# Hybrid attention block: gate weights prepared in a written order inside the last norm, and the norm's root in 128x1 pieces

## The chip, the cores and the metric

The kernel runs on one core of one Trainium2 chip. The metric is device microseconds of one execution. Five engines work side by side, each in its own program order: TensorE (matrix products, PE in the rows; its weight loads are PEld), VectorE (DVE), ScalarE (ACT), GpSimd (POOL) and SyncE (SP). Here SP does nothing but start loads, and POOL starts most stores.

## The reference, cut to what matters

One block: a mixer (short convolution and attention, merged and projected by `w_out`), then a SwiGLU feed-forward net. Each is normalised before and after. 1024 rows of 1024 columns, all float32.

```python
x = x + rmsnorm(m, norm_mix_post)            # m: the mixer's output
h = rmsnorm(x, norm_ffn_pre)
gu = einsum("bsd,df->bsf", h, w_gate_up)     # 1024 x 5632
g, u = split(gu, 2)
f = einsum("bsf,fd->bsd", silu(g) * u, w_down)
x = x + rmsnorm(f, norm_ffn_post)
```

`rmsnorm(x, g)` is `x * rsqrt(mean(x*x) + 1e-6) * g`, row by row.

## The kernel before, in words

**Products.** Each float32 operand is split into a high and a low part (`split`: ScalarE copies the high part, tile `hi`; VectorE subtracts it, tile `lo`), and a product is three matrix products, hi*hi, hi*lo and lo*hi (`mm3`). Each large product is a Strassen scheme over halves; `prod` is one of its terms: 4 blocks, 12 matrix products of 128x512.

**The place of the change.** After the mixer, the rows are worked off in four pairs of 128-row tiles (i = 0 to 3). `first`, `second`, `p_s1` to `p_a22` make the output of `w_out`; `e_norm(i)` does the post-norm, adds to x, stores x and does the pre-norm of the net; `e_turn(i)` transposes the two normalised tiles on TensorE (tile `tp`), and ScalarE copies them to `um`, from where `half_split` and `h2_sums` make the operands of the gate products. In `e_norm` the first tile of a pair lies in `raw` (pairs 0 to 2) or `keep` (pair 3), the second in `tt`. ScalarE squares each tile and sums it (`ssq`), then takes the root (`sq`); VectorE makes the inverse root of both tiles at once in `rms_finish`, on 128x2 values: a reciprocal, two multiplications, and a last step.

**The gate weights.** The columns of `w_gate` come in blocks of 128. Of eleven of them (`FIRSTS`, here called gate weights 0 to 10) the first two Strassen terms are done early, `f_begin` and `f_end`; this work stands around the last norm so that TensorE has something to do while VectorE normalises. The program writes `begin_early(0)`, `e_turn(2)`, `begin_early(1)`, `end_early(0)`, ..., `e_turn(3)`, then a loop over weights 4 to 10. A weight is loaded by SP into one of three `raw` buffers (weight 1 into `sx`), and split into `hi` and `lo`. The three `raw` buffers hold the pairs' tiles before, so a load waits until the buffer's last user is done:

```python
def raw_t():
    return wtile("raw", 3)
def prep_first(src1, there=None):
    if there is None:
        r1 = raw_t()
        nc.sync.dma_start(r1, kmaj(src1))
        h1, l1 = hi_t(), lo_t()
        split(h1, l1, r1)
```

In the loop, at weight 8, the lower half of the normalised rows is split into `hch` (ScalarE, in written order) and `hcl` (VectorE), four pieces each.

**What sets the order.** A scheduler orders each engine's instructions, except those that are made within `pinned(call, engine)` or under `strict[0]`: these are kept in the written order on that engine. The scheduler also decides which instructions of TensorE stand between others where they are not pinned. All work of VectorE and ScalarE goes through helpers, so every row of the profile says L77.

Of the kernel before, what the change touches and what calls it, by code (L numbers as in the profile page):

```python
# [13 lines left out]
ALU = mybir.AluOpType  # L14
# [33 lines left out]
def block_kernel(  # L48
# [20 lines left out]
    class InOrder:  # L69
# [15 lines left out]
    nc = SimpleNamespace(  # L85
        **{e: InOrder(e) for e in engines}
    )
# [22 lines left out]
    def add(o, a, b):  # L110
        nc.vector.tensor_tensor(o, a, b, op=ALU.add)

    def sub(o, a, b):
        nc.vector.tensor_tensor(o, a, b, op=ALU.subtract)
# [4 lines left out]
    def pinned(call, *names):  # L119

        was, strict[0] = strict[0], names
        call()
        strict[0] = was
# [5 lines left out]
    def copy(o, a):  # L129
        nc.scalar.activation(o, a, AF.Copy)  # L130

    def split(hi, lo, src):

        copy(hi, src)
        sub(lo, src, f32(hi))
# [9 lines left out]
    cpool, _ = pool("const")  # L145
    stat, _ = pool("stat", 4, side="right")
    stat.tile([P, 56], F32, name="pad", bufs=1)
    dpool, _ = pool("dram", space=DRAM)
# [34 lines left out]
    def rms_scale(ssq, rest=None, tile_=st_tile, w=1):  # L183
        return rms_finish(*rms_root(ssq, rest, tile_, w), tile_, w)

    def rms_root(ssq, rest=None, tile_=st_tile, w=1):

        va, sq = (tile_(n, w) for n in ("va", "sq"))
        eps = -0.5 * EPS if rest is None else rest[1]
        nc.vector.tensor_scalar(va, ssq, -0.5 / D, eps, op0=ALU.mult, op1=ALU.add)  # L190
        if rest is None:
            nc.scalar.activation(sq, va, AF.Sqrt, scale=-2.0)
        else:
            nc.scalar.activation(sq, ssq, AF.Sqrt, scale=1.0 / D, bias=rest[0])
        return va, sq
# [226 lines left out]
    op0, rest0 = upper(0, tp0)  # L422
# [36 lines left out]
    op1, rest1 = upper(1, tp1)  # L459
# [40 lines left out]
    for st in range(2, ST):  # L500
# [12 lines left out]
        if st + 3 == ST:  # L513
            ax_close()
            w0, w0_close = pool("w0", side="right")
            r0, h0, l0 = w0_tiles()
# [16 lines left out]
    wpool, _ = pool("w")  # L533
# [7 lines left out]
    def wtile(tag, bufs, dt=F32, shape=(P, KT, P)):  # L541
        return wpool.tile(list(shape), dt, tag=tag, name=tag, bufs=bufs)

    def raw_t():
        return wtile("raw", 3)

    def hi_t():
        return wtile("hi", 4, F32R)

    def lo_t():  # L550
        return wtile("lo", 3, F32R)
# [10 lines left out]
    def kmaj(src):  # L562
        return src.rearrange("(k p) m -> p k m", p=P)
# [3 lines left out]
# [7 lines that stand above are left out]
        else:  # L574
            r1, h1, l1 = there
        return dict(A11=(h1[:, LO], l1[:, LO]), A12=(h1[:, UP], l1[:, UP])), r1
# [469 lines left out]
    for ij, (kind, j, _, _) in enumerate(jobs):  # L1046
        work = side.pop(ij, [])

        def mid():
            for cut, _ in work:  # L1050
                pinned(cut, "vector", "scalar")
# [7 lines left out]
        if ij < 2:  # L1059
            if ij == 0:  # L1060
                r1 = raw_t()
# [13 lines left out]
            w = {**w, **prep_rest(wcols(jobs[ij][3]), r1)}  # L1075
            if ij == 1:
                pairs.q.append(pairs.prep(*pairs.srcs.popleft()))
            _, c12, c21, c22 = strassen(w, h1b, psm, pp, p1, mid)
        elif ij < len(jobs) - 1:
# [3 lines left out]
            w = pairs.get()  # L1083
# [3 lines left out]
        else:  # L1087
            w = pairs.get()
# [14 lines left out]
        elif kind == "gb":  # L1103
            for m, parts in ((j, (c11, c12)), (j + 1, (c21, c22))):
                zt = zts.pop(m)
                for n in range(2):
# [5 lines left out]
                    for t in (1, 0):  # L1112
# [5 lines left out]
                            op0=ALU.mult, op1=ALU.add,  # L1118
# [337 lines left out]
    PAIRS = ST // 2  # L1456
# [106 lines left out]
    for u in range(4):  # L1563
# [3 lines left out]
    late = [  # L1567
        x for t in (wtile("raw", 3), wtile("sx", 1)) for x in kept_halves(flat(t))
    ]
    late = {u: [gate(2 * u + 1 - x, n2, late.pop(0)) for x in range(2)] for u in (3, 0)}  # L1570
# [54 lines left out]
    gpr = bcast_row(norm_ffn_pre[0], ep, name="gpr")  # L1625

    def st2(name, bufs=2):
        return ep.tile([P, 2], F32, tag=name, name=name, bufs=bufs)

    def scale2(ssq):  # L1630
        return rms_scale(ssq, None, lambda n, w: st2(n), 2)

    def square(src, acc):
        junk = ep.tile([P, NC], F32, tag="junk", name="junk")
# [2 lines left out]
    sx = wtile("sx", 1)  # L1637
# [72 lines left out]
        prod(b1s[i], rests[i]["A22"], wob[T4], False)  # L1710
        square(b1s[i], qas[i][:, 1:2])

    def e_norm(i):
        qa = qas[i]
        add(qa, qa, qbs[i])
        rs = scale2(qa)
        tt = keeps[i], ep.tile([P, D], F32, tag="t", name="tt", bufs=1)
        xp = [xts.popleft() for _ in range(2)]
        ssq = st2("ssq")
        for e, parts in enumerate(  # L1720
            (((slice(0, D), keeps[i]),), ((n1, b1s[i]), (n2, c22s[i])))
        ):
            for ns, c in parts:
                nc.vector.scalar_tensor_tensor(
                    tt[e][:, ns], c, rs[:, e : e + 1], gpo[:, ns], op0=ALU.mult, op1=ALU.mult
                )
            add(xp[e], xp[e], tt[e])
            rows_ = slice((2 * i + e) * P, (2 * i + e + 1) * P)
            nc.gpsimd.dma_start(x2_dram[rows_, :], xp[e])
            nc.scalar.activation(tt[e], xp[e], AF.Square, accum_out=ssq[:, e : e + 1])  # L1730
        rs = scale2(ssq)
        for e in range(2):
            nc.vector.scalar_tensor_tensor(
                tt[e], xp[e], rs[:, e : e + 1], gpr, op0=ALU.mult, op1=ALU.mult
            )
            if 2 * i + 3 + e < ST:
                xts.append(load_xt(2 * i + 3 + e))
        turned.append(tt)
# [29 lines left out]
    def f_src(f):  # L1768
        return wgu[:, f * P : (f + 1) * P], wgu[:, FH + f * P : FH + (f + 1) * P]

    FIRSTS = [*range(2, NPRE), 0, 1]
    begun, kept, aside = {}, {}, {}

    def f_begin(n, b1, p1):
        f = FIRSTS[n]
        w, _ = prep_first(f_src(f)[0], aside.get(n))
        prod(b1, w["A11"], hb[B11], True)
        pinned(lambda: copy(p1, b1), *(("scalar",) if n >= 8 else ()))
        if f > 1:
            nc.gpsimd.dma_start(pre_dram[f][0], p1)  # L1780
        begun[n] = w, b1, p1
# [35 lines left out]
    for i in range(PAIRS):  # L1817
        if i + 1 < PAIRS:
            rests.append(rest_ops(i + 1))
        if i:  # L1820
            p_s1(i)
        p_s3(i)
        if i > 1:
            e_turn(i - 2, (0,))
        if i + 1 < PAIRS:
            p_s2(i + 1)
        if i > 1:
            e_turn(i - 2, (1,), (0,))
        if i == 3:
            p_a22(i)  # L1830
        if i > 1:
            e_turn(i - 2, (1,), (1,))
            half_split(B11, i - 2)
        if i == 2:
            hb.append(both(x_tile(2)))
        if i > 1:
            half_split(B21, i - 2)
        for p_ in ((p_a22, p_s4), (p_s4, p_a22), (p_s4, p_a22), (p_s4,))[i]:
            p_(i)
        e_norm(i)  # L1840
    hb.append(None)
    hb += [both(x_tile(n, p)) for n, p in ((0, wx), (3, wx), (4, wy), (5, wy))]
    r_, h_, l_ = wtile("sx", 1), hi_t(), lo_t()
    nc.sync.dma_start(r_, kmaj(f_src(FIRSTS[1])[0]))
    split(h_, l_, r_)
    aside[1] = r_, h_, l_
    sx = flat(wtile("sx", 1))
    early = [sx[:, n1], sx[:, n2], t_(fe, "c22"), t_(fe, "c22")]

    def begin_early(f):  # L1850
        if f == 2:
            raw_t()
        f_begin(f, pk.tile([P, NC], F32, tag="p1", name="b1"), early[f])

    def end_early(f):
# [605 lines left out]
```

## Time and profile before

| | |
|---|---|
| median of 3 runs | 1312.46 us (1311.39 to 1313.31) |
| profiled execution | 1312.72 us, its span 1311.0 us |
| granted clock of TensorE | 0.998 of full speed over the span |
| busy, share of the span | TensorE 99%, weight loads 83%, VectorE 74%, ScalarE 47%, GpSimd 12% |
| chain that ended last | TensorE 93%, VectorE 3%, DMA 2%, ScalarE 1% |

The stretch of the change lies between about 630 and 745 us of the span. From 650 to 745 us the page's rows show a full clock throughout. "Busy" of TensorE counts the modelled length of products that overlap, so waits shorter than an overlap don't show there; they show as the distance from one start to the next, which is 0.227 us where 128x512 products follow each other.

### The profile page before, as it was taken

To read this page: it belongs to the slowest core of one execution; us is meant where nothing else is said; L and a number is where in the kernel's file an instruction comes from. 1 tells how busy PE (TensorE), PEld (TensorE's weight loads), DVE (VectorE), ACT (ScalarE), POOL (GpSimd) and SP (SyncE) were. 2 spreads that over 40 slices of the span, in tenths; PEclk is the share of its full clock that TensorE was granted. 3 is DMA by queue.
4 is the path that set the end of the run, shared out by engine and by line. 5 is a ranking of instruction groups with operands and counts; after the bars stand their busy time and mean duration, and the time that the engine had idled before them with its cause. 6 is when DMAs were issued, how large, how long until landed. Compare 5 with 4: busy or idle time off the path is not lost.

```text
span 1311.0 us, 18265 instructions
## 1 busy us (share of the span) xinstructions
PE 1300.0 (99%) x6776; PEld 1087.4 (83%) x6776; DVE 964.0 (74%) x1501; ACT 611.0 (47%) x985; POOL 154.9 (12%) x289
## 2 busy tenths in 40 slices
PE   9999999999999999999999999999999999999997
PEld 8988888888888888888888888888888888888886
DVE  6975979875656877588798767777776667676685
ACT  6642423243355866454677434433343334444452
POOL 0001100011112222011012111211100110000000
PEclk9999999999999999999999999999999999999999
DMA  6347657668646544589466555543323338866441
GB/s 218 114 121 225 188 171 209 177 217 231 190 137 209 162 138 138 164 316 376 148 211 208 160 169 176 184 155 105 104 83 112 110 115 308 315 236 198 154 162 65
DMA packets 207242, 235.15 MB, mean 179 GB/s; under 512 B 12064, under 2 KB 150368, under 8 KB 207152
## 3 DMA queue, kind: packets, MB, share of 16 engines
q1 hardware_dynamic: 159136, 156.08, 37.8%
q0 software_dynamic: 18832, 63.22, 13.3%
q10 hardware_dynamic: 29184, 14.68, 4.5%
q8 instruction: 53, 0.87, 0.3%
q14 instruction: 37, 0.30, 0.1%
HBM read 161.79 MB, written 72.16 MB: 178 GB/s over the span
## 4 chain that ended last, share of the span: by engine, by line
PE 93%; DVE 3%; DMA 2%; ACT 1%; issue 1%; SPq 0%; DVEq 0%; ACTq 0%
PE b L77 54%; PE pd L77 16%; PE pba L77 3%; PE pv L77 3%; PE tps L77 3%; PE po L77 3%; PE p L77 2%; PE sp L77 2%; PE pbp L77 2%; PE pbv L77 1%; PE zb L77 1%; DMA xt<-in_x_dram 1%; PE ma L77 1%; PE q L77 1%; PE tp L77 1%
## 5 line engine op out<-in xcount | busy, mean ns | idle before, releaser
L77 PE MATMUL b<-x,hi 128*128 128x512 f32 x1088 | 335.6, 390 | 0.0
L77 PEld LDWEIGHTS b<-x,hi 128*128 128x128 f32 x1088 | 203.4, 188 | 42.0 <-ACT c L77 0.2
L77 PE MATMUL b<-x,lo 128*128 128x512 f32 x544 | 212.0, 390 | 0.0
L77 DVE TENSOR_TENSOR lo<-raw,hi 128x1024 fp32r<-128x1024 f32 (+1 forms) x89 | 107.1, 1203 | 48.6 <-PE b L77 39.4
L77 ACT ACTIVATE hi<-raw 128x1024 fp32r<-128x1024 f32 (+1 forms) x95 | 96.4, 1017 | 87.4 <-PE b L77 58.6
L77 PEld LDWEIGHTS b<-x,lo 128*128 128x128 f32 x544 | 102.1, 188 | 21.5 <-DVE lo L77 0.3
L77 DVE TENSOR_TENSOR c<-c,b 128x512 f32<-128x512 f32 x111 | 75.6, 682 | 29.6 <-PE b L77 21.3
L77 ACT ACTIVATE hi<-sx 128x1024 fp32r<-128x1024 f32 (+1 forms) x43 | 44.8, 1042 | 101.1 <-PE b L77 84.7
L77 DVE TENSOR_TENSOR sx<-raw 128x512 f32<-128x512 f32 x78 | 53.7, 688 | 24.8 <-DMA raw<-in_w_gate_up_dram 12.6
L77 DVE TENSOR_TENSOR lo<-sx,hi 128x1024 fp32r<-128x1024 f32 (+1 forms) x43 | 51.5, 1198 | 27.4 <-PE b L77 24.2
L77 PE MATMUL pd<-hi,lo 128*128 128x512 f32 x160 | 62.3, 389 | 0.0
L77 PE MATMUL pd<-hi 128*128 128x512 f32 x160 | 61.9, 390 | 0.0
L77 DVE TENSOR_TENSOR um<-um,b 128x512 f32<-128x512 f32 x47 | 31.9, 685 | 37.2 <-PE b L77 36.7
L77 PE MATMUL pd<-ghi 128*128 128x512 f32 x148 | 57.7, 390 | 0.0
L77 PE MATMUL pd<-glo,ghi 128*128 128x512 f32 x148 | 57.6, 389 | 0.0
L77 PE MATMUL pd<-ghi,glo 128*128 128x512 f32 x148 | 57.6, 389 | 0.0
L77 ACT ACTIVATE c<-b 128x512 f32<-128x512 f32 x49 | 28.9, 594 | 61.4 <-PE b L77 61.2
L77 PE MATMUL b<-hT34h,lo 128*128 128x512 f32 x136 | 52.9, 389 | 0.0
L77 PE MATMUL b<-hT12h,lo 128*128 128x512 f32 x136 | 52.9, 389 | 0.0
L77 PE MATMUL b<-hT34l,hi 128*128 128x512 f32 x136 | 52.9, 389 | 0.0
L77 PE MATMUL b<-hT12l,hi 128*128 128x512 f32 x136 | 52.9, 389 | 0.0
L77 PE MATMUL b<-hT34h,hi 128*128 128x512 f32 x136 | 52.9, 389 | 0.0
(505 smaller groups left out, 3166.2 us busy)
## 6 DMA issues: line engine op xcount, KB each, us to landing
raw<-in_w_gate_up_dram SPq DMA_DIRECT2D x54, 512.0 KB, 3.8
raw<-in_w_in_dram SPq DMA_DIRECT2D x35, 512.0 KB, 4.3
x<-wo_dram SPq DMA_DIRECT2D x28, 512.0 KB, 6.8
a_dramS<-um POOLq DMA_DIRECT2D x44, 256.0 KB, 2.6
a_dramA<-um POOLq DMA_DIRECT2D x33, 256.0 KB, 2.8
wo_dram<-h ACTq DMA_DIRECT2D x16, 448.0 KB, 4.4
wo_dram<-l ACTq DMA_DIRECT2D x16, 448.0 KB, 7.0
sg<-sg_dram SPq DMA_DIRECT2D x28, 256.0 KB, 3.0
```

Of the source, the lines that this page charges most:

```text
L77: ins = getattr(self.engine, name)(*args, **kw)
```

## The change

The root's inverse is now made in `scale2` itself: for the two tiles' columns apart, six instructions of 128x1 (reciprocal, product, last step, each for column 0 and then for column 1) instead of four of 128x2. `e_norm` takes two calls, `mid` and `late`, that are made between its steps; both post-norm products now come before the two additions to x; the pre-norm's end is pinned on VectorE for pairs 2 and 3. A new function, `weigh`, loads and splits one gate weight. Weights 1 and 0 are now written before the last pair's norm, 2 and 3 inside it (all of that norm is pinned on VectorE), and weights from 4 on are split under a pin on VectorE in `f_begin`.

```diff
     def scale2(ssq):
-        return rms_scale(ssq, None, lambda n, w: st2(n), 2)
+        va, sq = rms_root(ssq, None, lambda n, w: st2(n), 2)
+        r0, t0, r1 = (st2(n) for n in ("r0", "t0", "r1"))
+        each = [slice(e, e + 1) for e in range(2)]
+        for e in each:
+            nc.vector.reciprocal(r0[:, e], sq[:, e])
...
+        if mid:
+            mid()
+        for e in range(2):
             add(xp[e], xp[e], tt[e])
...
+        if late:
+            late()
+        def out():
+            rs = scale2(ssq)
...
+        pinned(out, *(("vector",) if i > 1 else ()))
...
+    def weigh(n, *pins, into=raw_t):
+        r, h, l = into(), hi_t(), lo_t()
+        nc.sync.dma_start(r, kmaj(f_src(FIRSTS[n])[0]))
+        pinned(lambda: split(h, l, r), *pins)
+        aside[n] = r, h, l
     def f_begin(n, b1, p1):
         f = FIRSTS[n]
-        w, _ = prep_first(f_src(f)[0], aside.get(n))
+        if n not in aside:
+            weigh(n, *(("vector",) if n > 3 else ()))
+        w, _ = prep_first(None, aside.pop(n))
...
-        e_norm(i)
+        if i < PAIRS - 1:
+            e_norm(i)
+    weigh(1, into=lambda: wtile("sx", 1))
+    weigh(0)
+    pinned(
+        lambda: e_norm(
+            PAIRS - 1, lambda: weigh(2, "vector"), lambda: weigh(3, "vector")
+        ),
+        "vector",
+    )
```

How the instructions move, at three places.

VectorE, in the norm of pair 2, before (`lo_6816` is the low part of gate weight 0; `raw_6189` is the pair's first tile, `x1` a half of the operand for TensorE):

```order
L77 TENSOR_TENSOR lo_6816<-raw_6813,hi_6815 128x1024
L77 TENSOR_TENSOR c22_6701<-c22_6701,b3_6676 128x512
L77 SCALAR_TENSOR_TENSOR raw_6189<-raw_6189,r1_6646,gpo_6064 128x1024
L77 TENSOR_TENSOR xt_6395<-xt_6395,raw_6189 128x1024
L77 TENSOR_TENSOR x1_6243<-um_3816,x1_6243 128x4x256
```

and now (`lo_6783` is weight 0's):

```order
L77 SCALAR_TENSOR_TENSOR raw_6189<-raw_6189,r1_6653,gpo_6064 128x1024
L77 TENSOR_TENSOR c22_6713<-c22_6713,b3_6688 128x512
L77 TENSOR_TENSOR xt_6399<-xt_6399,raw_6189 128x1024
L77 TENSOR_TENSOR lo_6783<-raw_6781,hi_6782 128x1024
L77 TENSOR_TENSOR x1_6243<-um_3816,x1_6243 128x4x256
```

The low part of weight 0, which frees the buffer of weight 3, moved behind three instructions.

ScalarE, a little later, before (`hi_6891` and `hi_6927` are the high parts of weights 2 and 3; `tt_6650,ssq_6651` is the square of pair 2's second tile):

```order
L77 ACTIVATE raw_6189,ssq_6651<-xt_6395 128x1024
L77 ACTIVATE x2_6606<-um_3816 128x4x256
L77 ACTIVATE hi_6891<-raw_6889 128x1024
L77 ACTIVATE tt_6650,ssq_6651<-xt_6518 128x1024
L77 ACTIVATE hi_6927<-raw_6925 128x1024
L77 ACTIVATE sq_6662<-va_6661 128x2
L77 ACTIVATE junk_6761,qb_6113<-keep_6204 128x512
```

and now (`hi_6807` and `hi_6819` are weights 2 and 3):

```order
L77 ACTIVATE hi_6807<-raw_6806 128x1024
L77 ACTIVATE x2_6614<-um_3816 128x4x256
L77 ACTIVATE hi_6819<-raw_6818 128x1024
L77 ACTIVATE tt_6660,ssq_6661<-xt_6527 128x1024
L77 ACTIVATE junk_6773,qb_6113<-keep_6204 128x512
L77 ACTIVATE sq_6672<-va_6671 128x2
L77 ACTIVATE sx_6843<-b1_6846 128x512
```

Both high parts now stand ahead of the square of the second tile, and another square (`junk`) ahead of the root.

VectorE, at weights 8 to 10 of the loop, before (`lo_7208`, `lo_7252`, `lo_7287` are weights 8, 9 and 10; `sx_7333` begins the next stage's weights):

```order
L77 TENSOR_TENSOR lo_7208<-raw_7205,hi_7207 128x1024
L77 TENSOR_TENSOR lo_7252<-raw_7249,hi_7251 128x1024
L77 TENSOR_TENSOR lo_7287<-raw_7284,hi_7286 128x1024
L77 TENSOR_TENSOR hcl_7013<-um_3816,hch_7012 128x4x128 x4
L77 TENSOR_TENSOR sx_7333<-raw_7329,raw_7331 128x512
```

and now (weights 9 and 10 are `lo_7266` and `lo_7301`):

```order
L77 TENSOR_TENSOR hcl_7028<-um_3816,hch_7027 128x4x128 x4
L77 TENSOR_TENSOR lo_7266<-raw_7264,hi_7265 128x1024
L77 TENSOR_TENSOR lo_7301<-raw_7299,hi_7300 128x1024
L77 TENSOR_TENSOR sx_7348<-raw_7344,raw_7346 128x512
L77 TENSOR_TENSOR raw_7346<-raw_7346 128x512
```

The low parts of weights 9 and 10 moved behind the four pieces of `hcl`. TensorE's order at the same place is now (`b1_7218` is another weight's product, 12 in all):

```order
L77 MATMUL b1_7263<-x1_6243,hi_7265 128x512 x2
L77 MATMUL b1_7218<-x2_6614,hi_7221 128x512 x2
L77 MATMUL b1_7218<-x2_6614,lo_7222 128x512
...
L77 MATMUL b1_7298<-x1_6243,hi_7300 128x512 x2
L77 MATMUL b1_7263<-x1_6243,lo_7266 128x512
```

where weight 9's twelve products stood together before: 16 products now lie between the first use of its high part and the first use of its low part, counted from the start of the former.

## Rows read from the trace of the kernel before

**Rows 1.** The page's first part: busy time, share and instructions of each engine.

```profile
PE 1300.0 (99%) x6776; PEld 1087.4 (83%) x6776; DVE 964.0 (74%) x1501; ACT 611.0 (47%) x985; POOL 154.9 (12%) x289
```

**Rows 2.** Timeline of TensorE: start, length (us), operation, count, idle before and releaser.

```profile
676.79 0.61 PE L77 MATMUL b<-x,hi 128*128 128x512 f32 x2
677.70 1.06 PE L77 MATMUL tp<-ident,raw 128*128 128x128 f32 x8 [0.29 <-DVE raw L77]
...
690.72 0.61 PE L77 MATMUL b<-x,hi 128*128 128x512 f32 x2
692.00 1.06 PE L77 MATMUL tp<-ident,keep 128*128 128x128 f32 x8 [0.67 <-DVE keep L77]
```

**Rows 3.** Timeline of VectorE, 664 to 683 us.

```profile
664.63 1.23 DVE L77 TENSOR_TENSOR lo<-raw,hi 128x1024 fp32r<-128x1024 f32 x1
...
668.83 1.22 DVE L77 TENSOR_TENSOR x<-um,x 128x1024 fp32r<-128x1024 f32 x1
...
675.48 0.16 DVE L77 RECIPROCAL r<-sq 128x2 f32<-128x2 f32 x1
675.56 0.14 DVE L77 TENSOR_TENSOR qa<-qa,qb 128x2 f32<-128x2 f32 x1
...
676.27 1.28 DVE L77 SCALAR_TENSOR_TENSOR raw<-xt,r,gpr 128x1024 f32<-128x1024 f32 x1
...
681.11 1.22 DVE L77 TENSOR_TENSOR xt<-xt,keep 128x1024 f32<-128x1024 f32 x1
682.24 0.74 DVE L77 SCALAR_TENSOR_TENSOR tt<-c,r,gpo 128x512 f32<-128x512 f32 x1
682.90 1.22 DVE L77 TENSOR_TENSOR lo<-raw,hi 128x1024 fp32r<-128x1024 f32 x1
```

**Rows 4.** Timeline of ScalarE, 672 to 676 us.

```profile
672.66 1.06 ACT L77 ACTIVATE tt<-xt 128x1024 f32<-128x1024 f32 x1
...
673.72 1.04 ACT L77 ACTIVATE hi<-raw 128x1024 fp32r<-128x1024 f32 x1
674.67 0.18 ACT L77 ACTIVATE sq<-va 128x2 f32<-128x2 f32 x1
674.76 0.62 ACT L77 ACTIVATE junk<-keep 128x512 f32<-128x512 f32 x1
...
675.95 0.21 ACT L77 ACTIVATE sq<-va 128x2 f32<-128x2 f32 x1
```

**Rows 5.** Timeline of SP's queue, 664 to 667 us.

```profile
665.19 1.11 SPq L77 DMA_DIRECT2D raw<-in_w_gate_up_dram  x2
```

**Rows 6.** DMA issues, 664 to 667 us: count, size, median us to landing.

```profile
raw<-in_w_gate_up_dram SPq DMA_DIRECT2D x2, 512.0 KB, 5.6
```

**Rows 7.** DMA issues, 697 to 711 us.

```profile
raw<-in_w_gate_up_dram SPq DMA_DIRECT2D x3, 512.0 KB, 4.9
```

**Rows 8.** DMA issues, 745 to 775 us.

```profile
raw<-in_w_gate_up_dram SPq DMA_DIRECT2D x5, 512.0 KB, 3.7
```

**Rows 9.** Timeline of TensorE, 722 to 742 us.

```profile
722.68 0.61 PE L77 MATMUL b<-x,hi 128*128 128x512 f32 x2
...
741.72 0.62 PE L77 MATMUL b<-x,hi 128*128 128x512 f32 x2
```

**Rows 10.** Timeline of ScalarE, 722 to 723 us.

```profile
722.93 0.60 ACT L77 ACTIVATE c<-b 128x512 f32<-128x512 f32 x1 [2.02 <-PE b L77]
```

**Rows 11.** Timeline of VectorE, 724 to 740 us.

```profile
724.08 2.49 DVE L77 TENSOR_TENSOR hcl<-um,hch 128x512 fp32r<-128x512 f32 x4
726.49 0.68 DVE L77 TENSOR_TENSOR sx<-raw 128x512 f32<-128x512 f32 x1
...
728.66 0.69 DVE L77 TENSOR_TENSOR s<-raw,sx 128x512 f32<-128x512 f32 x1
...
734.49 0.69 DVE L77 TENSOR_TENSOR sx<-raw 128x512 f32<-128x512 f32 x1 [2.39 <-DMA raw<-in_w_gate_up_dram]
...
739.92 0.68 DVE L77 TENSOR_TENSOR c<-um,b 128x512 f32<-128x512 f32 x1
```

More of the change, by code (lines that the diff above doesn't have):

```diff
@@ L1630, in scale2 @@
     def scale2(ssq):
-        return rms_scale(ssq, None, lambda n, w: st2(n), 2)
+        va, sq = rms_root(ssq, None, lambda n, w: st2(n), 2)
[3 more added lines that the diff above has]
+            nc.vector.reciprocal(r0[:, e], sq[:, e])
+        for e in each:
+            nc.vector.scalar_tensor_tensor(
+                t0[:, e], r0[:, e], va[:, e], r0[:, e], op0=ALU.mult, op1=ALU.mult
+            )
+        for e in each:
+            nc.vector.scalar_tensor_tensor(
+                r1[:, e], t0[:, e], 1.5, r0[:, e], op0=ALU.add, op1=ALU.mult
+            )
+        return r1
     def square(src, acc):
@@ L1711, in p_a22, with e_norm @@
         square(b1s[i], qas[i][:, 1:2])
-    def e_norm(i):
+    def e_norm(i, mid=None, late=None):
         qa = qas[i]
@@ L1730, in e_norm @@
             nc.scalar.activation(tt[e], xp[e], AF.Square, accum_out=ssq[:, e : e + 1])
-        rs = scale2(ssq)
+        if late:
+            late()
+        def out():
+            rs = scale2(ssq)
+            for e in range(2):
+                nc.vector.scalar_tensor_tensor(
+                    tt[e], xp[e], rs[:, e : e + 1], gpr, op0=ALU.mult, op1=ALU.mult
+                )
+        pinned(out, *(("vector",) if i > 1 else ()))
         for e in range(2):
-            nc.vector.scalar_tensor_tensor(
-                tt[e], xp[e], rs[:, e : e + 1], gpr, op0=ALU.mult, op1=ALU.mult
-            )
             if 2 * i + 3 + e < ST:
@@ L1839, in block_kernel @@
             p_(i)
-        e_norm(i)
+        if i < PAIRS - 1:
[7 more added lines that the diff above has]
+        "vector",
+    )
     hb.append(None)
     hb += [both(x_tile(n, p)) for n, p in ((0, wx), (3, wx), (4, wy), (5, wy))]
[L1843 to L1846, printed above, removed]
     sx = flat(wtile("sx", 1))
@@ L1850, in begin_early @@
     def begin_early(f):
-        if f == 2:
-            raw_t()
         f_begin(f, pk.tile([P, NC], F32, tag="p1", name="b1"), early[f])
```

## The prediction

> **What bounds the kernel now.** I read the page's busy table first: TensorE is busy for 99% of the span [rows 1], and the chain that ended last is almost all TensorE. So VectorE or ScalarE work counts only where TensorE stands still for it. The view of waits shows TensorE waiting for VectorE in the stretch of the change at two places alone, the transposes of the last two row pairs. The timeline tells their size, from start to start: two products at 0.227 us each are done 0.45 us after 676.79, at 677.24, and the transposes of pair 2 start at 677.70, a wait of 0.46; after 690.72 the same count gives 691.17, and pair 3's transposes start at 692.00, a wait of 0.83 [rows 2]. These 1.29 us are all that any better order can win here; the reader should keep that next to the 2.6 us (0.2%) that a measurement of this kernel can tell from nothing. So the question is which waits are made. The order of instructions, in the section on the change, shows three places.
>
> **The change part by part.** The 128x1 pieces: four instructions become six, in eight calls. Instructions that wait for nothing start 0.08 us after each other (675.48 and 675.56 [rows 3]), and the two columns alternate, so that each answer is there when it is wanted; by that step six take about 0.1 us less than four that wait for each other. I count it as nothing: a tenth on a chain is inside the errors below, and in the first two pairs TensorE never waits for VectorE.
>
> Here a rule speaks against the change. The Trainium skill (VectorE: DVE Perf Modes, "The DRAIN you can't avoid") says that a VectorE instruction starts only when the pipeline is empty, and its rules for authors say to keep the count of instructions small. By it six instructions would cost more than four, whatever their size. The two starts 0.08 us apart speak against it for small instructions without a wait; the sum would be 5.8 instead of 4.8 by the rule, which is the fourth rival below.
>
> Term A, transposes of pair 2. Weight 0's low part, which ended at 664.63 + 1.23 = 665.86, now stands last of the four instructions that take the time up to 668.83, so it ends near 668.85 [rows 3]. It frees the buffer into which SP loads weight 3. Before, that load was the second of the two of which the first went out at 665.19 [rows 5]; now it goes out near 668.85, and SP holds all later loads behind it. When it lands is the unknown price. The nearest loads of this size took 5.6 us (two at once [rows 6]), 4.9 (beside stores [rows 7]) and 3.7 (a quiet stretch [rows 8]). I take 4.9, since pair 2's store runs beside it and no second weight load; 3.7 and 5.6 are my bounds. It lands at 673.75. On ScalarE weight 3's high part now waits for it, and queued behind it are pair 2's second square, the other square and both roots, for which VectorE's pre-norm waits. The steps there [rows 4]: the high part takes 0.95 (673.72 to 674.67), so the square starts at 674.70 instead of 672.66; the square takes 1.06; the first root 0.09 (674.67 to 674.76); the other square and a copy 1.19 (674.76 to 675.95); from the second root to the pre-norm product 0.32 (675.95 to 676.27 [rows 3]). That product starts at 677.36; the transposes come 1.43 after it, as before (676.27 to 677.70), at 678.79. TensorE now reaches them two products earlier, at 676.79, and waits 2.00 instead of 0.46: +1.54. With 3.7 weight 3 lands at 672.55, but ScalarE has weight 2's high part (landed near 670.8) and a copy in front, 0.95 each, so that the high part starts near 672.7: +0.5. With 5.6: +2.25.
>
> Term B, weight 2's low part. It moved from ahead of the root to behind pair 3's two post-norm products. Their second, without the addition of 1.13 (681.11 to 682.24) ahead of it, starts 4.84 after the pre-norm product and takes 0.66 (682.24 to 682.90); the low part 1.22 [rows 3]; with 0.14 to TensorE (end 677.56 to 677.70) that is 6.86, or 5.43 after the transposes' start. TensorE has 16 transposes and 15 products until it wants it: 677.70 to 690.72 holds the transposes and 50 products, 13.02 us, which makes 1.7 for the former [rows 2] and 5.1 in all. +0.25, between 0 and 0.5.
>
> Term C, transposes of pair 3. They start 15.73 after pair 2's pre-norm product (676.27 to 692.00), since the last x tile is loaded when that product is done. From 677.36 this gives 693.09, and less where a low part that stood in that chain is gone. TensorE comes at 691.17 + 1.54 + 0.25 - 0.23 (one product fewer ahead) = 692.73. Of the 0.83 there remains 0 to 0.36: I take -0.8.
>
> Term D, weight 9's low part. It stands behind the four pieces of `hcl`, whose ScalarE halves wait for the end of the product that TensorE ends before 722.68. Before, `hcl` ran from 724.08 and the next instruction started at 726.49 [rows 11]; now the low part starts there, takes 1.23 (as at 664.63) and with 0.14 lets TensorE go on at 727.86. TensorE has 16 products of 0.227 (84 of them from 722.68 to 741.72 [rows 9]): done at 726.31. +1.55. No load is in it; the copy at 722.93 [rows 10] on which all hangs follows TensorE itself, so that earlier delays shift both sides alike.
>
> Term E, the next stage. The low part of term D also frees a buffer: the load behind it goes out at 727.75. With 4.9 it lands at 732.65; VectorE needs 2.86 (726.49 to 728.66, and 0.69) until the next buffer is free; the second load lands at 732.65 + 2.9 + 4.9 = 740.45. From the first subtraction on such a load to the end of the addition that frees the bank TensorE wants next took 734.49 to 740.60, 6.11, with a low part in it that now stands earlier (1.14: 1.23 less the 0.08 by which a next instruction starts before the end, as at 726.49): 4.97. So 745.42, with 0.14 at 745.56. TensorE, which came to that product at 741.72, comes at 741.72 + 1.55 = 743.27. +2.3. With 3.7 twice nothing is left; with 5.6 it is +3.7. After that a weight pair keeps TensorE for at least five terms of 12 products, 13.6 us, against two loads of 4.9, so I see no further wait.
>
> Sum: 1.54 + 0.25 - 0.8 + 1.55 + 2.3 = 4.8 us. The profiled execution took 1312.72 and would take 1317.5; the median of the runs is 0.26 below it, so I predict 1317.3. With the short loads: 0.5 + 0.25 - 0.8 + 1.55 = 1.5, 1314.0. With the long ones: 2.25 + 0.25 - 0.8 + 1.55 + 3.7 = 6.95, 1319.4.
>
> **The rivals.** First, quick loads: 1314.0, no change that can be told. For it: loads took 3.7 in a quiet stretch [rows 8]. Against: both loads run beside stores. The Trainium skill (DMA: Bandwidth & Descriptors, "Anatomy of one DMA — SWDGE (gpsimd) path") gives 2.0 us and 436 GB/s, an estimate of 3.2 us for 512 KB; by it A would stay at its floor, E would be nothing and the time 1314.0 too; all three rows here are longer.
>
> Second, on the other side: the written order does what an order can do, VectorE is done early with both pre-norms, and the 1.29 us of waits go: 1311.2. It needs weight 3's high part not to hold the square, so a load of under 672.66 - 0.95 - 668.85 = 2.9 us, and weight 9's low part in time, so that `hch` runs 1.55 us sooner after the copy. No row shows either.
>
> Third, crowded loads, 5.6 us each [rows 6]: 1319.4.
>
> Fourth, six small instructions cost 0.2 each in order: half a microsecond more on each of the two chains that end at transposes, 1318.3.
>
> **How the numbers follow.** The forecast, with loads of 4.2 to 5.4 us, gets 0.60 (1315.1 to 1319); quick loads 0.18, the other side 0.06, crowded loads 0.12, the drain 0.04. Slower by over 0.2% (above 1315.1): forecast, third and fourth, 0.76. Within 0.2%: first and second, 0.22, with 0.02 left for faster than 1309.8, since no row shows more than 1.29 us to win. The range of 8 in 10 takes in both bounds of the loads: 1313.6 to 1319.6; it leaves out the other side, and errors of the list of places.
>
> **What would show it.** In the profile after, pair 2's transposes should wait about 2 us behind the pre-norm product, with weight 3's high part on ScalarE ended by its load just before the second square; pair 3's should hardly wait; a product with `lo` should wait some 1.5 us at about 729 us, right behind `hcl`; and TensorE should stand once more near 746 us behind an addition of VectorE, with the loads of `raw` some 9 us later than before. If the first wait is under 1 us, the load was quick; if that near 729 is missing, term D is wrong and with it E; if waits show at places that I have not named, the list of places is wrong.

## The result, and the profile after

The changed kernel takes **1321.04 us** (median of 6 runs, 1319.89 to 1322.19), the kernel before 1311.89 in the same comparison (6 runs, 1311.39 to 1313.31): 9.15 us more, a ratio of 1.0068 with an interval of 1.0055 to 1.0081. The prediction was 1317.3, with 1313.6 to 1319.6 as its range. The sign was right; the loss is nearly twice the forecast, and the range did not hold it. The profiled execution took 1319.89 us with a span of 1318.1, 7.17 us more than the profiled one of before; it is the shortest of the six.

The page's first part, which answers to [rows 1]:

```profile
PE 1302.2 (99%) x6776; PEld 1089.2 (83%) x6776; DVE 964.5 (73%) x1517; ACT 610.9 (46%) x985; POOL 155.0 (12%) x289
```

VectorE has 16 more instructions and the same busy time (964.5 against 964.0 us), so no work was added. The view of TensorE's waits between 600 and 800 us (releaser: us in total, times, longest):

```profile
PE tp L77 <- DVE raw L77: 2.0, 1, 2.0
PE tp L77 <- DVE keep L77: 1.4, 1, 1.4
PE b L77 <- DVE lo L77: 1.3, 1, 1.3
PE b L77 <- ACT c L77: 1.0, 2, 0.7
PE b L77 <- DVE c L77: 0.8, 1, 0.8
```

Before there were two waits here, both at transposes [rows 2]. Now there are six, and the timeline of TensorE (start, length, operation, count, idle before) shows where:

```profile
676.03 0.39 PE L77 MATMUL b<-x,lo 128*128 128x512 f32 x1
678.42 1.58 PE L77 MATMUL tp<-ident,raw 128*128 128x128 f32 x8 [2.00 <-DVE raw L77]
...
680.23 1.91 PE L77 MATMUL tp<-ident,tt 128*128 128x128 f32 x8
...
694.53 1.07 PE L77 MATMUL tp<-ident,keep 128*128 128x128 f32 x8 [1.38 <-DVE keep L77]
...
707.93 0.73 PE L77 MATMUL b<-x,hi 128*128 128x512 f32 x2 [0.67 <-ACT c L77]
...
719.46 0.73 PE L77 MATMUL b<-x,hi 128*128 128x512 f32 x2 [0.35 <-ACT c L77]
...
732.83 0.50 PE L77 MATMUL b<-x,lo 128*128 128x512 f32 x1 [1.30 <-DVE lo L77]
...
749.35 0.74 PE L77 MATMUL b<-x,hi 128*128 128x512 f32 x2 [0.79 <-DVE c L77]
```

From start to start, as in the prediction (0.227 us for a product): 676.03 + 0.227 = 676.26, and pair 2's transposes start at 678.42, a wait of 2.16. In the same way the others are 1.54, 0.83, 0.51, 1.46 and 0.95; with 2.16 they make 7.45 us, against 1.28 before. One more thing stands in these rows: eight transposes that took 1.06 us [rows 2] take 1.58 and 1.91 here. The table by stretches (from and to, us, TensorE's busy time and count, granted clock, DMA share, GB/s) says why:

```profile
660.00:676.00 16.00, 16.00 (x80) 1.00 0.58 197
678.82:682.23 3.41, 3.41 (x17) 0.50 0.62 147
682.30:690.00 7.70, 7.70 (x35) 1.00 0.61 187
```

Behind the wait TensorE's granted clock is 0.50, that is 1.2 GHz in place of 2.4, for 3.41 us (from 678.82); then it is full again. What it costs can be read from another execution of the same kernel, experiment twelve, which had a full clock here: from the start of pair 2's transposes to the end of the last product ahead of pair 3's, the same 49 products and 16 transposes took 13.12 us there (678.76 to 691.88) and 14.57 here (678.42 to 692.99), so 1.45 us are lost. Waits and clock together: 7.45 - 1.28 + 1.45 = 7.62 us. The execution is 7.17 longer; TensorE came to the transposes of pair 2 at 676.26, half a microsecond ahead of the 676.79 that the rows of before gave, which makes up the rest. It is that far ahead from 407 us on, long before the place of the change.

**Where each wait begins.** VectorE's timeline, against [rows 3] and [rows 11]:

```profile
663.75 1.28 DVE L77 SCALAR_TENSOR_TENSOR raw<-raw,r,gpo 128x1024 f32<-128x1024 f32 x1
...
666.68 1.22 DVE L77 TENSOR_TENSOR lo<-raw,hi 128x1024 fp32r<-128x1024 f32 x1
...
677.00 1.27 DVE L77 SCALAR_TENSOR_TENSOR raw<-xt,r,gpr 128x1024 f32<-128x1024 f32 x1
...
683.50 1.22 DVE L77 TENSOR_TENSOR lo<-raw,hi 128x1024 fp32r<-128x1024 f32 x1
684.63 1.22 DVE L77 TENSOR_TENSOR xt<-xt,keep 128x1024 f32<-128x1024 f32 x1
...
693.10 1.28 DVE L77 SCALAR_TENSOR_TENSOR keep<-xt,r,gpr 128x1024 f32<-128x1024 f32 x1
...
729.14 2.50 DVE L77 TENSOR_TENSOR hcl<-um,hch 128x512 fp32r<-128x512 f32 x4 [6.76 <-ACT hch L77]
731.56 2.35 DVE L77 TENSOR_TENSOR lo<-raw,hi 128x1024 fp32r<-128x1024 f32 x2
737.50 0.69 DVE L77 TENSOR_TENSOR sx<-raw 128x512 f32<-128x512 f32 x1 [3.59 <-DMA raw<-in_w_gate_up_dram]
...
744.20 0.69 DVE L77 TENSOR_TENSOR sx<-raw 128x512 f32<-128x512 f32 x1 [0.46 <-DMA raw<-in_w_gate_up_dram]
...
748.62 0.68 DVE L77 TENSOR_TENSOR c<-um,b 128x512 f32<-128x512 f32 x1
```

SP's queue at four places, the loads of weights 3 and 4, against [rows 5], and the two loads of term E:

```profile
667.97 0.37 SPq L77 DMA_DIRECT2D raw<-in_w_gate_up_dram  x1
...
680.08 0.37 SPq L77 DMA_DIRECT2D raw<-in_w_gate_up_dram  x1
...
732.84 0.37 SPq L77 DMA_DIRECT2D raw<-in_w_gate_up_dram  x1
...
740.40 0.37 SPq L77 DMA_DIRECT2D raw<-in_w_gate_up_dram  x1
```

ScalarE's timeline, against [rows 4]:

```profile
673.43 1.06 ACT L77 ACTIVATE hi<-raw 128x1024 fp32r<-128x1024 f32 x1 [1.53 <-DMA raw<-in_w_gate_up_dram]
674.40 1.04 ACT L77 ACTIVATE tt<-xt 128x1024 f32<-128x1024 f32 x1
...
686.66 1.06 ACT L77 ACTIVATE hi<-raw 128x1024 fp32r<-128x1024 f32 x1 [3.89 <-DMA raw<-in_w_gate_up_dram]
...
688.10 1.05 ACT L77 ACTIVATE keep<-xt 128x1024 f32<-128x1024 f32 x1
...
705.75 0.60 ACT L77 ACTIVATE s<-b 128x512 f32<-128x512 f32 x1 [2.16 <-DMA pre_dram<-s]
```

The kernel before, weight 4's load and pair 3's first square:

```profile
675.64 0.37 SPq L77 DMA_DIRECT2D raw<-in_w_gate_up_dram  x1
```

```profile
682.81 1.04 ACT L77 ACTIVATE keep<-xt 128x1024 f32<-128x1024 f32 x1
```

Read the three together. Weight 0's low part ends at 667.90; weight 3's load goes out at 667.97; its high part starts at 673.43, 5.46 later, with pair 2's square right behind it at 674.40: the chain of the forecast's term A. The same happens a second time, unforeseen: weight 4's load goes out at 680.08, behind pair 2's transposes (before: at 675.64, behind weight 2's low part), its high part waits until 686.66, and pair 3's squares stand behind that, the first at 688.10 instead of 682.81. The tile that it squares was complete at 685.85 (684.63 + 1.22), so the load holds it for 2.25 us; the rest of the delay came earlier, on VectorE. Pair 3's pre-norm product is at 693.10. The third fact is the store at 705.75: the copy that TensorE awaits at 707.93 is queued behind one that waits for a store. (The other, at 719.46, is queued behind one that waits for a load, `c<-pre_dram`, until 716.99.)

### The profile page after: what moved, and what is told of

It is laid out like the page before. It is cut to its first block, busy times and chain, and to the rows that moved or that the text cites. A ratio compares the mean times of both kernels' runs of the same rounds, so it can differ in the third digit from the quotient of the medians.

```text
span 1318.1 us, 18284 instructions
## 1 busy us (share of the span) xinstructions
PE 1302.2 (99%) x6776; PEld 1089.2 (83%) x6776; DVE 964.5 (73%) x1517; ACT 610.9 (46%) x985; POOL 155.0 (12%) x289
## 4 chain that ended last, share of the span: by engine, by line
PE 91%; issue 3%; DVE 2%; DMA 2%; ACT 1%; POOL 0%; SPq 0%; DVEq 0%; POOLq 0%; ACTq 0%
PE b L77 52%; PE pd L77 16%; PE pba L77 3%; PE pv L77 3%; PE tps L77 3%; PE po L77 3%; PE p L77 2%; PE sp L77 2%; PE pbp L77 2%; DMA raw<-in_w_gate_up_dram 1%; PE pbv L77 1%; PE zb L77 1%; PE ma L77 1%; PE q L77 1%; PE mb L77 1%
## 5 line engine op out<-in xcount | busy, mean ns | idle before, releaser
L77 PE MATMUL b<-hT12h,hi 128*128 128x512 f32 x136 | 52.9, 389 | 0.0
```

Source lines behind the costliest of these rows:

```text
L77: ins = getattr(self.engine, name)(*args, **kw)
```

## The experiments

Each time is the median of its runs; differences are against the kernel before in the same comparison (1311.87 us for the first four, 1312.26 for the next four, 1312.08 for the last four), and "below the changed kernel" is below its 1321.04. Where no count is given, there were five runs.

**One: low parts of weights 5 to 10 free.**

```
-            weigh(n, *(("vector",) if n > 3 else ()))
+            weigh(n, *(("vector",) if n == 4 else ()))
```

> The changed kernel, but the low parts of weights 5 to 10 are no longer kept in the written order on VectorE (weight 4's still is). Theory one (terms D and E are real and separate): the wait of 1.46 us at the product with weight 9's low part, near 733 us, and the wait of 0.95 us near 749 us both go, the waits at the transposes and the half clock stay; 2.4 us less than the changed kernel, about 1318.6. Rival (what makes TensorE late is the chain of late loads, and waits only move from one place to the next): another wait of the same size takes their place before 760 us, and the time stays within 0.5 us of the changed kernel.

1319.21 us (1318.22 to 1321.37), ratio 1.0058 (1.0045 to 1.0070): 1.8 below the changed kernel. Both waits near 733 and 749 us are gone, as theory one has it. But others moved in its profiled execution (at 1321.37 the longest of its runs): 2.09 at pair 2's transposes, 2.81 at pair 3's, 1.96 at 711, with the clock at half behind the last two. So D and E are real, and the earlier waits vary by more than expected from one execution to the next; the 1.8 us are less than the 2.4 expected.

**Two: the old root.**

```
     def scale2(ssq):
-        va, sq = rms_root(ssq, None, lambda n, w: st2(n), 2)
-        ...
-        return r1
+        return rms_scale(ssq, None, lambda n, w: st2(n), 2)
```

> The changed kernel with the root's products of before (four instructions on 128x2 columns in place of six on 128x1). Theory one (the pieces cost nothing by themselves, but they move what stands beside them): in the order that comes of it ScalarE has pair 2's second square ahead of weight 3's high part again, with only the root behind it; the wait at pair 2's transposes falls from 2.16 us to about 0.6, so the half clock behind it (about 1.7 us) does not come; together 3.2 us less, about 1317.8, if pair 3's wait stays as it is. Rival one (the small instructions cost their empty pipeline): only the two short chains get shorter, by 0.5 us each at most, 1320.0 to 1320.5, with the wait of 2 us and the half clock still there. Rival two (the prediction's: the pieces are worth nothing in any way): within 0.3 us of the changed kernel.

1314.80 us (11 runs, 1314.54 to 1315.71), ratio 1.0023 (1.0014 to 1.0032): **6.2 us below the changed kernel**, twice what theory one had, and far from both rivals. VectorE's timeline shows what the edit moved:

```profile
663.78 1.23 DVE L77 TENSOR_TENSOR lo<-raw,hi 128x1024 fp32r<-128x1024 f32 x1
...
665.52 1.28 DVE L77 SCALAR_TENSOR_TENSOR raw<-raw,r,gpo 128x1024 f32<-128x1024 f32 x1
```

Weight 0's low part is ahead of the post-norm product again, as in [rows 3]. The waits at the transposes are 0.27 and 0.20 us, under the 0.45 and 0.83 of before; those on copies and the half clock are gone. What is left is term D, 1.46 us, and term E, 2.10 us:

```profile
726.80 0.50 PE L77 MATMUL b<-x,lo 128*128 128x512 f32 x1 [1.30 <-DVE lo L77]
...
744.72 0.74 PE L77 MATMUL b<-x,hi 128*128 128x512 f32 x2 [1.94 <-DVE c L77]
```

**Three: weight 3's high part behind pair 2's square and root.** `issue_after` queues what is written under it behind one instruction of the same engine; `last[2]` is the root of pair 2.

```
-        pinned(lambda: split(h, l, r), *pins)
+        behind = last.get({3: 2}.get(n))
+        with tc.issue_after(behind.ins) if behind else ExitStack():
+            copy(h, r)
+        pinned(lambda: sub(l, r, f32(h)), *pins)
```

> The changed kernel with one thing else on ScalarE: weight 3's high part stands behind pair 2's second square and its root instead of ahead of both. Theory one (term A is the load that holds the square): no wait at pair 2's transposes, or under 0.3 us, no half clock behind it, the transposes near 676.3; pair 3's transposes then come as soon as their own chain lets them, which is led by weight 4's load (sent out when pair 2's transposes have read their buffer), so TensorE waits longer there, 2 to 3 us instead of 1.54; in all 2 to 3 us less than the changed kernel, about 1318.4. Rival (the square was late for another reason, or the half clock comes without the wait): transposes of pair 2 near 678, or the half-clock stretch still there, less than 1 us won.

1317.87 us (1317.28 to 1319.50), ratio 1.0046: 3.2 below the changed kernel. The first wait fell from 2.16 to 0.53 (I had under 0.3), the clock stayed full, and pair 3's wait is 1.66 (I had 2 to 3), hardly other than the changed kernel's 1.54. So what made the square late was that load. The waits on copies (0.87 and 0.53) and those of D and E (1.46 each) are still there.

**Four: 18 transposes that nobody reads, ahead of pair 2's.**

```
                 def turns():
+                    if (i, e, q) == (2, 0, 0):
+                        for k in range(18):
+                            nc.tensor.transpose(tp[:, k % 4, :], ident, ident)
```

> The changed kernel with 18 transposes of the identity, which nothing reads, ahead of pair 2's first transposes, in the bank that these then overwrite: TensorE works for 1.8 of the 2.16 us in which it stood still. Theory one (TensorE fell to half its clock because it stood still): no stretch at half clock near 679 us, the transposes at 0.1 us each, and the products up to 690 us some 1.7 us earlier than in the changed kernel, with the transposes starting at the same time, 678.4; the end some 1 to 2 us earlier if pair 3's transposes do not swallow it, since that wait of 1.54 us can grow by as much. Rival (the clock falls for what TensorE does there, or by the hour): the stretch at half clock is still there, and nothing is won.

1318.36 us (1317.57 to 1318.82), ratio 1.0049. It did not do what it was made for: the scheduler put the 18 two products ahead of the wait, which stayed whole, and it also moved weight 4's high part behind pair 3's squares, so that pair 3's wait is gone. It tells one thing of the clock all the same: the wait of 2.17 us (2.00 in the row) was *not* followed by half a clock here.

```profile
675.34 0.71 PE L77 MATMUL b<-x,hi 128*128 128x512 f32 x2
678.05 1.09 PE L77 MATMUL tp<-ident,raw 128*128 128x128 f32 x8 [2.00 <-DVE raw L77]
```

**Five: the kernel before with the new root alone.** `scale2` as in the change, nothing else.

> The kernel before with one edit: the root's products in two 128x1 chains. In the order that comes of it weight 0's low part moves behind pair 2's first post-norm product and an addition, and ScalarE has weight 3's high part ahead of pair 2's second square and the root, as in the whole change; weights 2 and 5 to 10 stay as before. Theory one (the pieces' own cost is nothing, what they shift is the loss): a wait of some 2 us at pair 2's transposes instead of 0.45, half a clock after it in some executions (up to 1.7 us), a longer wait at pair 3's; 2 to 4 us above before, 1314 to 1316. Rival (the prediction's reading: the pieces are nothing, term A comes from the order written by hand): the time of before, 1311.9, within 0.5 us. Second rival (an empty pipeline for each small instruction): 0.5 to 1 us above before, with no wait over 1 us.

1313.96 us (11 runs, 1312.71 to 1315.64), ratio 1.0015 (1.0006 to 1.0024): 1.7 above before. Weight 0's low part is the late one again, the wait at pair 2's transposes is 1.60, and ScalarE shows the reason:

```profile
673.66 1.06 ACT L77 ACTIVATE hi<-raw 128x1024 fp32r<-128x1024 f32 x1 [0.69 <-DMA raw<-in_w_gate_up_dram]
674.62 1.04 ACT L77 ACTIVATE tt<-xt 128x1024 f32<-128x1024 f32 x1
```

But pair 3's transposes do not wait at all; I had expected a longer wait there. With weight 2's low part in its old place, weight 4's load is on time. The loss is a little under my 2 to 4, and its profiled execution (1313.42) accounts for little of it: the waits add 0.32 us to those of before, and the span is 0.7 us longer. Where the rest of the 1.7 lies, no row shows.

**Six: the new root, but weight 0's low part ahead of the post-norm products.**

```
+        if i == 2:
+            weigh(1, into=lambda: wtile("sx", 1))
+            weigh(0)
+            ahead_of[2] = nc.vector.last.ins
         if i < PAIRS - 1:
             e_norm(i)
-    weigh(1, into=lambda: wtile("sx", 1))
-    weigh(0)
...
-                nc.vector.scalar_tensor_tensor(
+                with tc.issue_after(ahead_of[i]) if i in ahead_of else ExitStack():
+                    nc.vector.scalar_tensor_tensor(
```

> The changed kernel with its new root, but weight 0's low part held ahead of pair 2's post-norm products on VectorE (the post-norm products are queued behind it). ScalarE's order then has the square of pair 2 ahead of weight 3's high part, as before. Theory one (one misplaced low part is the cause of term A, of the half clock and of what follows at pair 3 and at the two copies): the time of the changed kernel with the old root, 1314.8, within 0.5 us, although the new root stays; waits left near 727 and 745 us, 1.5 and 2.1 us. Rival (the small instructions themselves cost it): the changed kernel's 1321.0, or at most 1 us below.

1315.10 us (7 runs, 1314.58 to 1316.58), ratio 1.0028 (1.0017 to 1.0038): 5.9 below the changed kernel, with every instruction of the new root in place. VectorE and ScalarE:

```profile
663.64 1.23 DVE L77 TENSOR_TENSOR lo<-raw,hi 128x1024 fp32r<-128x1024 f32 x1
...
665.38 1.28 DVE L77 SCALAR_TENSOR_TENSOR raw<-raw,r,gpo 128x1024 f32<-128x1024 f32 x1
```

```profile
671.93 1.05 ACT L77 ACTIVATE tt<-xt 128x1024 f32<-128x1024 f32 x1
...
672.97 1.04 ACT L77 ACTIVATE hi<-raw 128x1024 fp32r<-128x1024 f32 x1
```

The square is ahead of weight 3's high part, and the waits left are 0.53 and 0.68 at the transposes, 1.46 (term D) and 1.24 (term E, where I had 2.1). This is the run that decides: two thirds of the loss hang on the place of one low part, 1.22 us long, and on what the scheduler places differently with it.

**Seven and eight: two versions without the losses.** Seven is the edits of one and two together (old root, low parts of weights 5 to 10 free); eight is those of one and six (new root).

> The changed kernel with the old root, and with the low parts of weights 5 to 10 free: only the written order around pair 3's norm is left of the change. Theory one: the waits of 1.46 and 2.1 us near 727 and 745 us go, those at the two sets of transposes stay at 0.3 and 0.2 us (1.28 together in the kernel before); 3.5 us under the version with the old root alone, 1311.2, which is 0.6 under the kernel before. Rival (with these waits gone, others show, as the loads follow each other): 1312.5 to 1314.

> The changed kernel with its new root, weight 0's low part held ahead of pair 2's post-norm products, and the low parts of weights 5 to 10 free. The same order on every engine as the version with the old root and free low parts, so that the two differ by the root's instructions alone. Theory one: 1311.2, and within 0.3 us of that version. Rival (an empty pipeline for each small instruction): 0.5 to 1 us above that version.

1311.93 us (11 runs, 1311.26 to 1314.53), ratio 1.0000 (0.9991 to 1.0009), and 1312.22 (11 runs, 1311.66 to 1313.00), ratio 1.0002 (0.9993 to 1.0011). The waits at the two sets of transposes are 0.27 and 0.21 us in seven, 0.37 and 0.39 in eight, against 0.45 and 0.83 before; a new one at a low part takes 0.27 and 0.19 of it back. Neither can be told from the kernel before: the written order around pair 3's norm wins at most some tenths, and seven lies between theory one's 1311.2 and the rival's 1312.5. The two versions differ by 0.3 us. Their order is not quite the same, as the expectation has it: from 687 us on some of ScalarE's copies and of TensorE's products stand elsewhere (the high part at 688.15 in seven is ahead of pair 3's root, the one at 689.29 in eight behind it). So the 0.3 us is not the root's alone; it leaves no room for the 0.5 to 1 us of an empty pipeline at each small instruction.

**Nine: weight 2's low part free and early.**

```
+    weigh(2)
     pinned(
         lambda: e_norm(
-            PAIRS - 1, lambda: weigh(2, "vector"), lambda: weigh(3, "vector")
+            PAIRS - 1, None, lambda: weigh(3, "vector")
```

> The changed kernel, but weight 2 is prepared ahead of pair 3's norm with its low part free, as in the kernel before, so that its buffer is given up near 675 us and weight 4's load gets it, instead of the buffer that pair 2's transposes give up at 680. Theory one (pair 3's transposes were late because weight 4's load was, and its high part stands ahead of pair 3's squares on ScalarE): that high part no longer waits for its load, the wait at pair 3's transposes falls from 1.54 us to between 0 and 0.7, and 1 to 1.5 us are won, 1319.5 to 1320; the wait of 2 us at pair 2's stays. Rival (pair 3's chain is led by its last x tile): the wait stays at 1.5 us or more, and the time at 1321.

1318.11 us (1315.96 to 1318.36), ratio 1.0041: 2.9 below the changed kernel. Weight 4's load goes out at 676.42, its high part waits for no load, and the wait at pair 3's transposes is gone, as they stand right behind a product of 692.87:

```profile
693.10 1.03 PE L77 MATMUL tp<-ident,keep 128*128 128x128 f32 x8
```

The change also drops a bare `raw_t()` call ahead of weight 2, which let one buffer's turn pass; nine lacks that call too, so it is not what makes the load late. A wait of 0.77 us on another copy came in at 678.62. The gain is more than the 1 to 1.5 us expected; the clock is full in the profiled execution, and the first wait 1.60.

**Ten: weight 4's high part behind pair 3's squares and root.** The edit of three, with `{4: 3}` in place of `{3: 2}`.

> The changed kernel with weight 4's high part behind pair 3's squares and root on ScalarE instead of ahead of them; its load comes as late as in the changed kernel. Theory one: the load holds nobody, pair 3's transposes wait 0 to 0.5 us instead of 1.54, and 1.5 to 2.5 us are won, 1318.5 to 1319.5; the wait of 2 us at pair 2's stays, with or without the half clock. Rival (led by the last x tile): the wait stays at 1.5 us, and the time at 1321.

1318.39 us (1314.50 to 1319.21), ratio 1.0039: 2.7 below. Pair 3's wait is gone although the load is as late as ever (679.98), the transposes standing right behind a product of 693.02; pair 2's wait is 2.16, with half a clock behind it.

```profile
693.25 1.03 PE L77 MATMUL tp<-ident,keep 128*128 128x128 f32 x8
```

**Eleven: the version of seven, with both high parts behind the roots.** The edits of seven and of three, with `{3: 2, 4: 3}`.

> The version with the old root and free low parts, and in it the high parts of weights 3 and 4 behind the squares and roots of pairs 2 and 3. Theory one: the waits of 0.27 and 0.2 us at the transposes go too, 0.4 us less than without this, 1311.5, about 0.5 under the kernel before, which five rounds can hardly tell. Rival (the high parts, now later, hold TensorE at the products with weights 3 and 4): 0.5 to 2 us more.

1312.72 us (11 runs, 1312.18 to 1313.80), ratio 1.0005 (0.9996 to 1.0014): nothing won. The waits at the transposes are still 0.41 and 0.24, and one of 0.76 on a copy of ScalarE came at 703, behind a copy that waited for a store. The rival was nearer.

**Twelve: the changed kernel once more.**

> The changed kernel itself once more. Theory one (the half clock is a consequence of the wait of 2 us at pair 2's transposes, but not in every execution): 1321, with waits of 2 and 1.5 us at the two sets of transposes again, and the stretch at half clock there or not. Rival (the stretch belongs to the program at that place): it starts again near 679 us.

1320.85 us (1319.89 to 1321.77), ratio 1.0064. In this profiled execution (1321.45) the first wait is 1.60 and pair 3's is 2.69, and the half clock stands behind the second. TensorE by stretches, behind the one and the other:

```profile
679.00:682.00 3.00, 3.00 (x22) 1.00 0.65 117
695.30:698.50 3.20, 3.20 (x15) 0.50 0.28 106
```

So the stretch at half clock belongs to no place in the program; it follows a long wait.

## Why the prediction was wrong

| step | predicted | measured | verdict |
|---|---|---|---|
| A, transposes of pair 2 | +1.54 | 2.16 - 0.45 = +1.71 | right, in part by luck |
| B, weight 2's low part | +0.25 | 0 | small |
| C, transposes of pair 3 | -0.8 | 1.54 - 0.83 = +0.71 | **wrong, other sign** |
| D, weight 9's low part | +1.55 | +1.46 | right |
| E, next stage | +2.3 | +0.95 | loads shorter than priced |
| TensorE's clock | no term | +1.45 | **missing** |
| copies on ScalarE | no term | 0.83 + 0.51 = +1.34 | **missing** |
| sum | 4.84 | 7.62 | |

**The step that failed is term C**: "They start 15.73 after pair 2's pre-norm product [...], since the last x tile is loaded when that product is done." In the changed kernel that chain does not end last: the x tile's load went out at 678.68 and took 4.5 us, and pair 3's squares started at 688.10. Term A followed what weight 0's low part gives up; term B moved weight 2's low part later in just the same way and priced only the wait for its values, not the buffer that it holds. Weight 4's load then went into the buffer that pair 2's transposes give up, at 680.08 instead of 675.64, and ScalarE held pair 3's squares behind it. Nine (the load early again) and ten (the load late, but nobody behind it) each take the wait away, so both links of this chain are shown. From that high part to pair 3's transposes it is 7.87 us here (686.66 to 694.53), 7.87 in twelve and 7.88 in three, so the wait's size hangs on the load: 6.58 us from its issue to the high part here, 6.80 in twelve, where the wait is 2.69. In two and six the load goes out just as soon after pair 2's transposes, but takes 5.49 and 5.83, TensorE has 2 and 4 products more to do in between, and the waits are 0.20 and 0.68. Term A is not what makes C: in three its wait is down to 0.53, and pair 3's is still 1.66. The root alone cost 1.7 us (five), the order without it 2.9 us, which is D and E (two, seven), and both together 9.15. The 4.5 us more are about what neither shows alone in its rows: the wait at pair 3, the half clock and the waits on copies, 1.54 + 1.45 + 1.34 = 4.33.

**Term A** came closer than its parts. The low part ended 0.95 sooner than forecast (667.90 against 668.85), the load took 5.46 in place of 4.9, and TensorE came 0.53 sooner (676.26 against 676.79); these partly cancel. In twelve the same wait is 1.60, which makes the term 1.15.

**What the sum had no term for.** The waits of A and C were taken at face value. A half-clock stretch behind one adds 1.45 us. And ScalarE, once late, has its copies behind others that wait for a store (705.75) or a load (716.99). By the prediction's own sign, waits at places that it had not named, its list of places was wrong. That these waits are a consequence is shown by six: with weight 0's low part early one of 0.18 us is left of them.

**Term E** was forecast with the right chain, but each of its two loads at 4.9 us. The first went out at 732.84 and was used at 737.50, 4.66 later; the second at 740.40 and 744.20, 3.80 later. That is 1.34 us less, and the term is 1.35 smaller than forecast. The other runs bear it out: in two the loads took 6.13 (726.80 to 732.93) and 3.73, and the wait is 2.10; in six 5.03 and 3.74, and 1.24; in nine 4.18 and 3.80, and 0.50.

**The 128x1 pieces.** Their own cost was counted as nothing, and that holds to within 0.3 us (seven and eight). The fourth rival made 1 us of it. VectorE at pair 3's root, seven and then eight:

```profile
679.34 0.17 DVE L77 RECIPROCAL r<-sq 128x2 f32<-128x2 f32 x1 [0.74 <-ACT sq L77]
...
680.12 1.28 DVE L77 SCALAR_TENSOR_TENSOR keep<-keep,r,gpo 128x1024 f32<-128x1024 f32 x1
```

```profile
678.85 0.23 DVE L77 RECIPROCAL r<-sq 128x1 f32<-128x1 f32 x2 [0.55 <-ACT sq L77]
...
679.52 1.28 DVE L77 SCALAR_TENSOR_TENSOR keep<-keep,r,gpo 128x1024 f32<-128x1024 f32 x1
```

From the first reciprocal to the product that uses the root it is 0.78 us without the pieces and 0.67 with them. Each column's chain is also a step shorter now, three instructions in place of four, as the two multiplications are one. By the Trainium skill (VectorE: DVE Perf Modes, "The DRAIN you can't avoid") a VectorE instruction starts only when the pipeline is empty, and the same paragraph adds that one which is not held starts earlier. The six in eight go with the addition: they start 0.11 us apart on average. What the prediction did not ask is whose term A is; it is the doing of the new root and not of the written order: with it the scheduler puts weight 0's low part, which no rule holds, behind the post-norm product; five shows it without the rest of the change, two and six show it undone. The order after the change was read rightly, so term A was right; whose it was is seen by building the parts apart. Why four instructions or six tip the scheduler is not shown.

**The rivals.** Weight 3's load took 5.46 us (667.97 to a high part at 673.43), near the long bound, weight 4's 6.58, beyond it, and the two of term E 4.66 and 3.80: no one price held. The crowded loads' time, 1319.4, was the nearest, for a different reason. Seven comes near the other side, but with most of the change undone.

**What stays open.** When the clock falls. In the profiled executions eight waits of TensorE between 660 and 760 us were 1.96 us or longer. The two longest (2.69 and 2.81) were followed by, or ended in, half a clock, and so were three of the six between 1.96 and 2.17; none of those up to 1.66 was. Only the profiled executions have rows, but each run has its mean granted clock on record, to three places. It is 0.997 in 7 of the 11 runs of the changed kernel, and never that low in 59 of the kernel before. The median of those 7 is 1321.5 us, that of the other 4 is 1320.3, though one of the 7 is the shortest of all. So the stretch comes in most of its runs and is likely part of their spread of 2.3 us; more is not shown. Filling the wait with work was tried once (four) and missed it.

## What to carry to other kernels

When an instruction moves, follow two things that it releases: its values and its buffer; then look at what stands behind the load into that buffer on an engine that works in order. An edit without cost of its own can still move unpinned neighbours, so build each part of a change alone and compare the orders before adding up the whole. A load has no one price either: here 512 KB took 3.7 to 6.9 us. And a long wait at the bounding engine should be priced above its length, as its clock may fall behind it: it did at five of the eight longest waits here, for some 1.45 us each.

## What the runs showed of the hardware that I had not expected

- TensorE's granted clock went to 0.50 for 3.41 us behind some waits of about 2 us, and came back by itself: in all five stretches seen mid-kernel the length was the same. Eight transposes then took 1.58 to 1.91 us instead of 1.06. In one execution it followed the wait at 678.42, in another of the same kernel that at 694.57.
- A load of 512 KB took 6.6 us (out at 680.08, high part at 686.66) beside the load of an x tile and a store; before, three such loads beside stores took 4.9 in the median [rows 7]. The wait at pair 2's transposes, which ends such a chain, was 2.16 us in one execution of the changed kernel and 1.60 in another.
- Six instructions on 128x1 that take turns start 0.11 us apart on average (678.85 to 679.52 in eight), four on 128x2 that need each other's answer 0.20 (679.34 to 680.12 in seven).
